# Two-layer hybrid encoder on one core: transposes of the heads' probabilities in runs of eight, a second value buffer, a second bank for the memory's products, later row classes in branch B, contiguous x

## The chip, the cores and the metric

The kernel runs on one core of a Trainium2 chip. TensorE (PE) multiplies and transposes, VectorE (DVE), ScalarE (ACT) and GpSimd (POOL) do the elementwise work, SyncE (SP) and ScalarE issue most DMAs. The metric is the device time of one execution in microseconds; lower is better.

## The reference

The reference is two layers of an encoder over 512 tokens of width 1024, float32, with 256 memory tokens that are normalised once and used by both layers.

```
mem_n = rms_norm(mem, mem_norm_g)
for l in range(DEPTH):                       # DEPTH = 2
    h = rms_norm(x, g_pre_mix[l])
    q_a,k_a,v_a, q_b,k_b,v_b, q_m, gate_pre = split(h @ w_in[l])
    o_a = neighborhood_attention(q_a, k_a, v_a, rpb_na[l])   # 6 heads of 64, windows of 8 x 16
    o_b = dilated_attention(q_b, k_b, v_b)                   # 3 groups of 2 heads, mixed by denominators
    o_m = memory_attention(q_m, mem_n, w_mem_kv[l])          # 4 heads, 256 memory tokens
    gates = sigmoid(gate_pre + b_gate[l])
    merged = gates[0]*(o_a @ w_br_a[l]) + gates[1]*(o_b @ w_br_b[l]) + gates[2]*(o_m @ w_br_m[l])
    x = x + rms_norm(merged @ w_out[l], g_post_mix[l])
    u = depthwise_conv(rms_norm(x, g_pre_ffn[l]) @ w_up[l])  # width 3, D_FF = 2816
    a, b = split(u)
    x = x + rms_norm((gelu(a) * b) @ w_down[l], g_post_ffn[l])
```

## The kernel before, in words

All activations lie transposed, channels on partitions: x is eight tiles of 128 channels by 512 tokens, in two halves of 256 tokens. A float32 product is made of three products of rounded parts: each weight tile `wraw` and each activation is split in a high part (a CAST on ScalarE: `whi`, `h_111`, `m`) and a low part (a subtraction on VectorE: `wlo`, `h_112`), and TensorE adds hi·hi, hi·lo and lo·hi in one PSUM bank. In the listings h with odd numbers 111 to 125 are the high parts of the eight normalised channel tiles and the even ones their low parts; `h_95`, `h_97` and so on with a second number are tiles in which x is scaled before the split.

The banks of PSUM are pools: three "mm" banks for products, two "s" banks for scores, two "pt" banks for transposes (`tbank`), one "o" bank for a head's values. A tile of a pool waits until the instructions that read the bank's last tile are done. The same holds for buffers in SBUF: "sq" (line 324, 585, 674) is one buffer, in which `a_v` and `b_v` put a value tile before it is transposed.

The program is written by a small planner, the class `Woven`. It counts a nominal clock `clk` of TensorE's work. Attention heads, normalisations and value transposes are generators ("jobs") that are spawned with a delay. A job yields a number (the nominal microseconds until its next part is due) or a flag that it needs. While a projection is written, `tick` runs every job that is due. So the yields set where a job's parts stand between the projection's products, and TensorE executes strictly in the written order. The other engines execute in the order in which their instructions were placed, too, so a part that is placed earlier stands ahead of others on every engine. `ready(t)` makes the yield at least as long as the nominal backlog of ScalarE and VectorE.

Layer 0 begins with `load_x` for both halves (256 KB per DMA, line 196), a first group of six projection tiles for each half (`run_group`: half 0 first, then half 1, 48 products of 0.12 us for each pair of tiles), and the jobs `pre_norm_job` (half 1 with delay `SD1`) and `mem_norm_job` (delay 6.0). The latter loads the memory (line 460, on ScalarE's queue), squares it on ScalarE (`sq`), and adds the squares on VectorE; the sum goes through a product with a column of means. `mem_kv` then makes keys and values of the memory in four tiles. In the second layer its weights were loaded ahead (`pre`).

Branch A is six `a_head_job`s in each layer: scores of four windows in two parts, softmax (ScalarE's exponential, VectorE's RECIPROCAL and TENSOR_SCALAR), then eight 128 x 128 transposes of the probabilities `y` into two pt banks, each emptied by a CAST on ScalarE and a subtraction on VectorE, then the products with the values into the o bank. Branch B is four `b_job`s in each layer (two heads, two pairs of row classes): each class makes scores in both s banks, then three runs of four transposes follow. Branch M is four `m_head_job`s with two runs of four.

## Time and profile before

| | |
|---|---|
| time, median of 3 runs | 1542.07 us (1540.83 to 1543.23) |
| the profiled execution | 1541.12 us, its span 1539.3 us |
| TensorE busy | 1518.5 us, 99% of the span, 7970 products and transposes |
| VectorE, ScalarE, GpSimd busy | 941.2, 713.2 and 122.9 us |
| DMA | 149.23 MB, 97 GB/s over the span |
| granted TensorE clock | 0.998 |

In rows of the timeline the first number is the start in us from the span's beginning, the second the duration, then engine, line, operation, output<-inputs, shape, count; in brackets the idle time before it and whose work ended it. Line 114 is a helper through which all ScalarE and VectorE work is issued, line 252 issues all products, line 263 all transposes.

### The profile page before, as it was taken

The page shows a single profiled execution, that of the slowest core. Times are in us where ns is not written, and L with a number is a line of the kernel's source. Part 1 is how long each engine was busy: PE and PEld are TensorE (multiplying, and loading weights), DVE is VectorE, ACT ScalarE, POOL GpSimd, SP SyncE. Part 2 cuts the span into 40 slices and gives each one's busy share as a digit, 9 for nine tenths or more (in the row PEclk, how much of TensorE's full clock was granted, in tenths as well). Part 3 has the DMA queues.
Part 4 walks back from the last instruction along what each step waited for, and adds up shares of the span by engine and source line. Part 5 has one row for each costly group of instructions (what it writes and reads, how often), then busy time and mean ns, then how long its engine had stood idle before and what let it go on. Part 6 is the DMA issues. An engine that isn't in the chain of part 4 may idle for free.

```text
span 1539.3 us, 20627 instructions
## 1 busy us (share of the span) xinstructions
PE 1518.5 (99%) x7970; PEld 1297.4 (84%) x7970; DVE 941.2 (61%) x1686; ACT 713.2 (46%) x1272; POOL 122.9 (8%) x191
## 2 busy tenths in 40 slices
PE   8999999999999999999999999999999999999997
PEld 7988888888988888888898888888889888888887
DVE  6685676335777777633387856743457877776233
ACT  5565554235544444533366655533355544444231
POOL 3220000220000000010044100012100000000000
PEclk9999999999999999999999999999999999999999
DMA  7331113224212222333362221132350233223331
GB/s 254 95 110 62 62 57 100 92 95 153 67 56 96 96 97 96 120 100 97 116 178 81 85 71 57 59 116 75 116 164 15 90 100 98 96 96 90 99 104 64
DMA packets 47490, 149.23 MB, mean 97 GB/s; under 512 B 5648, under 2 KB 9872, under 8 KB 47392
## 3 DMA queue, kind: packets, MB, share of 16 engines
q1 hardware_dynamic: 43632, 139.46, 28.4%
q0 software_dynamic: 2464, 6.36, 1.7%
q10 hardware_dynamic: 1296, 2.10, 0.4%
q8 instruction: 62, 1.02, 0.3%
q14 instruction: 36, 0.29, 0.1%
HBM read 145.80 MB, written 2.10 MB: 96 GB/s over the span
## 4 chain that ended last, share of the span: by engine, by line
PE 94%; DVE 3%; ACT 1%; issue 1%; DMA 0%; SPq 0%; ACTq 0%
PE mm L252 82%; PE s L252 5%; PE o L252 4%; PE pt L263 2%; PE pt L252 1%; DVE m L114 1%; DVE y L114 1%; DVE ka L114 0%; DMA x<-in_xT_dram 0%; ACT y L114 0%; DVE wlo L114 0%; DVE h L114 0%; DVE st L114 0%; ACT whi L114 0%; PE pt L347 0%
## 5 line engine op out<-in xcount | busy, mean ns | idle before, releaser
L252 PE MATMUL mm<-h,whi 128*128 128x512 f32 x2496 | 775.6, 392 | 0.0
L252 PEld LDWEIGHTS mm<-h,whi 128*128 128x128 f32 x2496 | 461.5, 188 | 91.0
L252 PE MATMUL mm<-h,wlo 128*128 128x512 f32 x1248 | 486.5, 390 | 0.0
L114 DVE TENSOR_TENSOR wlo<-wraw,whi 128x1024 fp32r<-128x1024 f32 (+1 forms) x213 | 258.3, 1213 | 284.7 <-ACT whi L114 282.0
L114 ACT CAST whi<-wraw 128x1024 fp32r<-128x1024 f32 (+1 forms) x213 | 221.1, 1038 | 307.8 <-PE mm L252 292.9
L252 PEld LDWEIGHTS mm<-h,wlo 128*128 128x128 f32 x1248 | 234.2, 188 | 49.7
L252 PE MATMUL mm<-m,whi 128*128 128x512 f32 (+1 forms) x800 | 215.1, 356 | 0.9 <-DVE m L114 0.8
L252 PEld LDWEIGHTS mm<-m,whi 128*128 128x128 f32 x800 | 141.8, 189 | 22.8 <-PE mm L252 1.3
L252 PE MATMUL mm<-m,wlo 128*128 128x512 f32 (+1 forms) x400 | 142.2, 355 | 0.0
L114 DVE SCALAR_TENSOR_TENSOR y<-y,vec,y 128x511 f32<-128x511 f32 x176 | 130.4, 747 | 3.5 <-ACT y L114 0.9
L114 DVE TENSOR_TENSOR y<-mm,R 128x512 f32<-128x512 f32 x82 | 56.3, 687 | 68.5 <-PE mm L252 68.5
L252 PEld LDWEIGHTS mm<-m,wlo 128*128 128x128 f32 x400 | 75.5, 189 | 10.9
L114 ACT ACTIVATE y<-y,vec 128x512 f32<-128x512 f32 x88 | 71.0, 813 | 2.1 <-DVE y L114 1.9
L804 POOL TENSOR_TENSOR m<-m,y 128x512 f32<-128x512 f32 x28 | 36.1, 1288 | 399.5 <-DVE y L114 399.5
L252 PE MATMUL mm<-m,m 128*128 128x512 f32 x240 | 63.5, 394 | 0.0
L114 ACT ACTIVATE y<-y 128x512 f32<-128x512 f32 x44 | 27.8, 632 | 72.0 <-DVE y L114 71.5
L114 ACT CAST m<-pt 128x512 fp32r<-128x512 f32 (+1 forms) x72 | 38.5, 540 | 46.2 <-PE pt L263 36.3
L114 DVE TENSOR_TENSOR m<-pt,m 128x512 fp32r<-128x512 f32 (+1 forms) x72 | 45.0, 629 | 20.7 <-ACT m L114 19.5
L114 ACT ACTIVATE y<-y,st 128x256 f32<-128x256 f32 (+1 forms) x80 | 43.6, 546 | 28.6 <-DVE st L114 25.8
L114 DVE TENSOR_TENSOR acc<-acc,sq 128x256 f32<-128x256 f32 (+1 forms) x80 | 38.1, 477 | 26.3 <-ACT sq L114 24.4
L114 ACT CAST m<-y 128x512 fp32r<-128x512 f32 x32 | 19.8, 619 | 72.5 <-DVE y L114 72.5
L114 DVE TENSOR_TENSOR m<-wraw,m 128x512 fp32r<-128x512 f32 (+1 forms) x60 | 38.4, 653 | 22.8 <-ACT m L114 22.7
(157 smaller groups left out, 1765.4 us busy)
## 6 DMA issues: line engine op xcount, KB each, us to landing
wraw<-in_w_in_dram SPq DMA_DIRECT2D x88, 512.0 KB, 3.7
wraw<-in_w_up_dram SPq DMA_DIRECT2D x88, 512.0 KB, 3.7
wraw<-in_w_down_dram SPq DMA_DIRECT2D x32, 512.0 KB, 3.5
wraw<-in_w_out_dram SPq DMA_DIRECT2D x16, 512.0 KB, 4.2
wraw<-in_w_down_dram SPq DMA_DIRECT2D x16, 384.0 KB, 3.2
wraw<-in_w_kv_dram SPq DMA_DIRECT2D x8, 512.0 KB, 4.1
y<-in_rpb_dram POOLq DMA_DIRECT2D x12, 256.0 KB, 3.5
wraw<-in_w_bra_dram SPq DMA_DIRECT2D x16, 192.0 KB, 2.3
```

The costliest lines, as they stand in the source:

```text
L114: return op(*args, **kw)
L252: wv.pe(nc.tensor.matmul(ps, a, b, start=first, stop=last), cost)
L263: wv.pe(nc.tensor.transpose(ps[:, 128 * i:128 * i + 128], s, ident), 0.11)
L804: (V if br == 2 and m >= 6 else G).tensor_add(acc[m], acc[m], gs)
```

## The change

Seven edits. `SD1`, the delay of half 1's normalisation job, goes from 4.0 to 5.0. x is laid out so that each 256 KB DMA reads one contiguous piece of DRAM (before: 128 rows of 2 KB, 16 KB apart). The "sq" pool gets two buffers. Odd tiles of the memory's keys and values go to a pt bank in layer 0. In `a_head_job` and `m_head_job` there is no yield between the two runs of transposes. In `b_job` the second row class yields at least the backlog of the engines, and there is no yield behind the first run of transposes.

```diff
--- before.py
+++ after.py
@@ -36,7 +36,7 @@
 LAT_QK, LAT_SM, LAT_T, LAT_V, LAT_T2 = 1.0, 4.5, 1.5, 2.0, 0.6
 STEP_A, STEP_B, STEP_M = 9.0, 9.0, 5.5
 SQG, LOG, GEN, KVE = {0: (), 1: ()}, {0: (), 1: ()}, 'DVVGVG', 'VVDD'
-SD1 = 4.0
+SD1 = 5.0
 MARGIN = 0.3
 SB = True
 TAILG = (0, 2, 4, 6)
@@ -193,7 +193,7 @@
     def load_x(half):
         for k in range(0, KD, 2):
             i = half.start // 256
-            nc.sync.dma_start(out=xs[:, i, k:k + 2, :], in_=xT[:, i, k:k + 2, :])
+            nc.sync.dma_start(out=xs[:, i, k:k + 2, :], in_=xT[i, k // 2])
 
     g0 = const.tile([128, KD], F32, name="g0")
     nc.scalar.dma_start(out=g0, in_=vecs[:, 0, V_PRE:V_PRE + KD])
@@ -321,7 +321,7 @@
             ACT.activation(acc, src, AF.Square)
         else:
             n = acc.shape[-1]
-            sq = slot((128, 256)) if slot else small("sq2", 4) if n == 256 else small("sq", 1, (128, 512))
+            sq = slot((128, 256)) if slot else small("sq2", 4) if n == 256 else small("sq", 2, (128, 512))
             ACT.activation(sq, src, AF.Square)
             (eng or V).tensor_add(acc, acc, sq)
 
@@ -485,7 +485,7 @@
         wv.need(f"mem{l}")
         for m in range(4):
             w = pre[m] if pre else weights(w_kv[l, m], KD, 128)
-            ps = mmbank((128, N_MEM))
+            ps = (mmbank if pre or m % 2 == 0 else tbank)((128, N_MEM))
             linear(ps, w, hm, slice(0, N_MEM))
             if m < 2:
                 t, u = big(F32R, (128, 2, N_MEM)), big(F32R, (128, 2, N_MEM))
@@ -582,7 +582,7 @@
 
     def a_v(ps, qkv, flag):
 
-        vT = small("sq", 1, (128, 512))
+        vT = small("sq", 2, (128, 512))
         ps3 = ps.rearrange("p (r c) -> p r c", r=8)
         vv = vT.rearrange("p (j r c) -> p j r c", j=4, r=8)
         ACT.copy(vv[:, 1:4], ps3[:, :, 8:56].rearrange("p r (j c) -> p j r c", j=3))
@@ -623,7 +623,6 @@
             yield LAT_QK if bp == 0 else ready(LAT_SM)
         c0, c1 = slice(0, 128), slice(128, 256)
         t0 = transpose_split([P[0][:, c0], P[3][:, c1], P[0][:, c1], P[1][:, c0]])
-        yield ready(LAT_T2)
         t1 = transpose_split([P[1][:, c1], P[2][:, c0], P[2][:, c1], P[3][:, c0]])
         yield ready(LAT_T)
         po = obank(128)
@@ -671,7 +670,7 @@
         qkv[1].append(kk)
 
     def b_v(g, ps, qkv, flag):
-        vT = small("sq", 1, (128, 512))
+        vT = small("sq", 2, (128, 512))
         if g == 0:
             ACT.copy(vT, ps)
         else:
@@ -706,12 +705,13 @@
             V.tensor_scalar_mul(S1[:, c2, :], S1[:, c2, :], d0)
             P.append([S[:, 128 * i:128 * i + 128] for i in range(4)]
                      + [S1[:, c2, 128 * i:128 * i + 128] for i in range(2)])
-            yield LAT_QK if c2 == 0 else ready(LAT_SM)
+            yield ready(LAT_QK if c2 == 0 else LAT_SM)
         tt = []
         for i in range(3):
             tt.append((transpose_copy if i == 2 else transpose_split)(
                 [P[c2][2 * i + a] for a in range(2) for c2 in range(2)]))
-            yield ready(LAT_T2) if i < 2 else ready(LAT_T)
+            if i > 0:
+                yield ready(LAT_T2 if i == 1 else LAT_T)
         for kt in range(4):
             off = 256 * (kt % 2)
             mm_values(po, vs[0][kt][sl], [t[:, off:off + 256] for t in tt[kt // 2]],
@@ -755,7 +755,8 @@
         tt = []
         for kt in range(2):
             tt.append(transpose_split([P[q][:, 128 * kt:128 * kt + 128] for q in range(4)]))
-            yield ready(LAT_T2) if kt == 0 else ready(LAT_T)
+            if kt == 1:
+                yield ready(LAT_T)
         po = obank(128)
         for kt in range(2):
             mm_values(po, vm[pr][:, kt, h % 2], tt[kt], lambda t: t, kt == 0, kt == 1, 512)
@@ -1066,7 +1067,7 @@
         return v.reshape(L, -1, 128)
 
     a = {}
-    a["xT"] = np.ascontiguousarray(g["x"][0].T.reshape(KD, 128, 2, 256).transpose(1, 2, 0, 3))
+    a["xT"] = np.ascontiguousarray(g["x"][0].T.reshape(4, 2, 128, 2, 256).transpose(3, 0, 2, 1, 4))
     a["memT"] = np.ascontiguousarray(g["mem"][0].T.reshape(KD, 128, N_MEM).transpose(1, 0, 2))
     a["memg"] = np.ascontiguousarray(g["mem_norm_g"].reshape(KD, 128).T)
     vec = np.concatenate([cols(g["g_pre_mix"]), cols(g["g_post_mix"]), cols(g["g_pre_ffn"]), cols(g["g_post_ffn"]),
```

The numbers of instructions on each engine are the same as before. What moves is the order. On ScalarE, in the first 40 us, the casts of half 1's high parts (h_115 to h_125) stood between the memory's loads and ahead of its squares (sq, from m tiles 385 to 391):

```order
L114 CAST h_119<-h_87_369 128x256
L460 DMA m_387<-in_memT_dram 128x512
L460 DMA m_389<-in_memT_dram 128x512
L114 CAST h_121<-h_88_373 128x256
L114 CAST h_123<-h_89_377 128x256
L114 CAST h_125<-h_90_381 128x256
L460 DMA m_391<-in_memT_dram 128x512
L114 ACTIVATE h_95_393<-m_385 128x256
L114 ACTIVATE sq_96_395<-m_385 128x256
L114 ACTIVATE sq_97_398<-m_387 128x256
L114 ACTIVATE sq_98_401<-m_387 128x256
```

After the change the same stretch reads:

```order
L114 ACTIVATE sq_89_364<-m_353 128x256
L114 ACTIVATE sq_90_367<-m_353 128x256
L114 ACTIVATE sq_91_370<-m_355 128x256
L114 ACTIVATE sq_92_373<-m_355 128x256
L114 ACTIVATE sq_93_376<-m_357 128x256
L114 CAST h_111<-h_95_390 128x256
L114 ACTIVATE sq_94_379<-m_357 128x256
L114 CAST h_113<-h_96_394 128x256
L114 CAST whi_700<-wraw_698 128x1024
L114 CAST whi_741<-wraw_739 128x1024
L114 CAST h_115<-h_97_398 128x256
L114 CAST h_117<-h_98_402 128x256
```

The memory's four loads and eight squares now stand ahead of the second half's casts, and two weight casts (whi, for the memory's keys) between them. VectorE in the same stretch, before; h_122 to h_126 are low parts of half 1, the rows with h_95_393 add up the memory's squares:

```order
L114 TENSOR_TENSOR h_122<-h_88_373,h_121 128x256
L114 TENSOR_TENSOR h_124<-h_89_377,h_123 128x256
L114 TENSOR_TENSOR h_126<-h_90_381,h_125 128x256
L114 TENSOR_TENSOR h_95_393<-h_95_393,sq_96_395 128x256
L114 TENSOR_TENSOR h_95_393<-h_95_393,sq_97_398 128x256
L114 TENSOR_TENSOR h_95_393<-h_95_393,sq_98_401 128x256
L114 TENSOR_TENSOR h_95_393<-h_95_393,sq_99_404 128x256
L114 TENSOR_TENSOR h_95_393<-h_95_393,sq_100_407 128x256
L114 TENSOR_TENSOR h_95_393<-h_95_393,sq_101_410 128x256
L114 TENSOR_TENSOR h_95_393<-h_95_393,sq_102_413 128x256
L114 TENSOR_TENSOR wlo_701<-wraw_698,whi_700 128x1024
L114 TENSOR_TENSOR wlo_742<-wraw_739,whi_741 128x1024
```

And after; the memory's sum is now h_87_359, and scalings of x (SCALAR_TENSOR_TENSOR) and low parts follow behind:

```order
L114 TENSOR_TENSOR h_112<-h_95_390,h_111 128x256
L114 TENSOR_TENSOR h_87_359<-h_87_359,sq_92_373 128x256
L114 TENSOR_TENSOR h_114<-h_96_394,h_113 128x256
L114 TENSOR_TENSOR h_87_359<-h_87_359,sq_93_376 128x256
L114 SCALAR_TENSOR_TENSOR h_97_398<-x,g_86,pt_337 128x256
L114 TENSOR_TENSOR h_87_359<-h_87_359,sq_94_379 128x256
L114 SCALAR_TENSOR_TENSOR h_98_402<-x,g_86,pt_337 128x256
L114 TENSOR_TENSOR wlo_701<-wraw_698,whi_700 128x1024
L114 TENSOR_TENSOR h_116<-h_97_398,h_115 128x256
L114 TENSOR_TENSOR h_118<-h_98_402,h_117 128x256
L114 SCALAR_TENSOR_TENSOR h_99_406<-x,g_86,pt_337 128x256
L114 SCALAR_TENSOR_TENSOR h_100_410<-x,g_86,pt_337 128x256
```

Of half 1 two low parts (h_112, h_114) now stand among the memory's sums, and h_116 to h_126 behind the first subtraction of memory weights, wlo_701, some also behind the second, wlo_742.

The second place is the first layer's head 0 on VectorE: y_1012 and y_1036 are its four probability tiles, m_1106 the low part of its first bank of transposes. Before:

```order
L114 TENSOR_SCALAR y_1012<-y_1012,st_1021 128x256
L114 TENSOR_SCALAR y_1036<-y_1036,st_1039 128x256
L114 RECIPROCAL st_1045<-st_1045 128x1
L114 TENSOR_SCALAR y_1036<-y_1036,st_1045 128x256
L114 SCALAR_TENSOR_TENSOR ka_1054<-mm_965,ka_1052 64x512
L114 TENSOR_TENSOR wlo_1119<-wraw_1116,whi_1118 128x1024
L114 SCALAR_TENSOR_TENSOR ka_1055<-mm_965,ka_1053 64x512
L114 TENSOR_TENSOR m_1106<-pt_1100,m_1105 128x512
```

After:

```order
L114 TENSOR_SCALAR y_1012<-y_1012,st_1021 128x256
L114 TENSOR_SCALAR y_1036<-y_1036,st_1039 128x256
L114 SCALAR_TENSOR_TENSOR ka_1054<-mm_965,ka_1052 64x512
L114 TENSOR_TENSOR wlo_1128<-wraw_1125,whi_1127 128x1024
L114 RECIPROCAL st_1045<-st_1045 128x1
L114 SCALAR_TENSOR_TENSOR ka_1055<-mm_965,ka_1053 64x512
L114 TENSOR_SCALAR y_1036<-y_1036,st_1045 128x256
L114 TENSOR_TENSOR m_1106<-pt_1100,m_1105 128x512
L114 TENSOR_TENSOR m_1115<-pt_1109,m_1114 128x512
```

The last normalisation (RECIPROCAL and TENSOR_SCALAR with st_1045) now stands behind a key and a weight subtraction, and the two banks of transposes, pt_1100 and pt_1109, are emptied one directly after the other.

The third place is TensorE at the last job of branch B in layer 0: y_2284 and y_2331 hold the probabilities of its row classes, y_2283 the rest of them, o_2181 takes the values. Before:

```order
L263 MATMUL pt_2400<-ident,y_2284 128x128
L263 MATMUL pt_2400<-ident,y_2331 128x128
L263 MATMUL pt_2400<-ident,y_2284 128x128
L263 MATMUL pt_2400<-ident,y_2331 128x128
L252 MATMUL mm_2411<-m_1190,m_2317 128x512
L252 MATMUL mm_2411<-m_1191,m_2317 128x512
L252 MATMUL mm_2411<-m_1190,m_2318 128x512
L252 MATMUL mm_2411<-m_1438,m_2317 128x512
L252 MATMUL mm_2411<-m_1439,m_2317 128x512
L252 MATMUL mm_2411<-m_1438,m_2318 128x512
L263 MATMUL pt_2418<-ident,y_2283 128x128 x4
L252 MATMUL mm_2411<-m_1660,m_2317 128x512
```

After, with y_2311, y_2353 and y_2310 in the same parts:

```order
L252 MATMUL mm_2393<-m_1658,m_2278 128x512
L252 MATMUL mm_2393<-m_1657,m_2279 128x512
L263 MATMUL pt_2403<-ident,y_2311 128x128
L263 MATMUL pt_2403<-ident,y_2353 128x128
L263 MATMUL pt_2403<-ident,y_2311 128x128
L263 MATMUL pt_2403<-ident,y_2353 128x128
L263 MATMUL pt_2412<-ident,y_2311 128x128
L263 MATMUL pt_2412<-ident,y_2353 128x128
L263 MATMUL pt_2412<-ident,y_2311 128x128
L263 MATMUL pt_2412<-ident,y_2353 128x128
L263 MATMUL pt_2422<-ident,y_2310 128x128 x4
L252 MATMUL o_2181<-m_2408,m_1472 128x256
```

The three runs of transposes stood apart, with products between them; now twelve stand in one run, on two pt banks.

## The prediction

> **What bounds the kernel now.** I read the page first: busy time, the slices, the chain.
>
> ```profile
> PE 1518.5 (99%) x7970; PEld 1297.4 (84%) x7970; DVE 941.2 (61%) x1686; ACT 713.2 (46%) x1272; POOL 122.9 (8%) x191
> PE 94%; DVE 3%; ACT 1%; issue 1%; DMA 0%; SPq 0%; ACTq 0%
> ```
>
> TensorE is busy for 99% of the span and 94% of the chain, and the change removes none of its products. So what can be won is TensorE's idle time, 1539.3 − 1518.5 = 20.8 us, and what can be lost is new idle time. A table of windows says where it lies (start:end, length, then busy time of each engine, granted clock, DMA share, GB/s):
>
> ```profile
> 0.00:17.00 17.00, 11.76 (x35) 7.99 (x35) 7.39 (x18) 8.48 (x20) 5.42 (x34) 1.00 0.80 269
> 17.00:36.00 19.00, 18.07 (x141) 17.87 (x142) 15.59 (x37) 12.57 (x33) 7.70 (x8) 1.00 0.75 267
> 36.00:62.00 26.00, 25.16 (x210) 24.98 (x210) 16.74 (x33) 12.78 (x27) 7.79 (x13) 1.00 0.21 66
> 62.00:135.00 73.00, 72.06 (x405) 61.80 (x404) 57.18 (x151) 47.07 (x110) 14.94 (x24) 1.00 0.32 102
> 135.00:222.00 87.00, 86.14 (x459) 71.48 (x458) 49.94 (x113) 42.57 (x83) 0.00 (x0) 1.00 0.21 65
> ...
> 780.00:895.00 115.00, 112.80 (x733) 101.65 (x733) 92.11 (x229) 69.26 (x162) 33.77 (x65) 1.00 0.33 102
> 895.00:1006.00 111.00, 109.94 (x589) 91.38 (x588) 73.76 (x172) 59.06 (x129) 0.00 (x0) 1.00 0.19 60
> 1006.00:1515.00 509.00, 509.00 (x2509) 431.75 (x2507) 286.20 (x400) 210.47 (x307) 18.03 (x14) 1.00 0.30 95
> 1515.00:1540.00 25.00, 15.76 (x131) 15.35 (x130) 10.48 (x31) 2.02 (x6) 3.20 (x4) 0.89 0.26 85
> ```
>
> Start (5.2 us idle) and tail (9.2, of which 0.7 is behind the span's end) hold two thirds. The second layer's gate and MLP stage idles 0.0 us in 509 (the first layer's, left out, reads alike). The attention stages, which nearly all of the edits touch, idle 0.84 + 0.94 + 0.86 + 2.20 + 1.06 = 5.9 us. That caps what the attention edits can win at about 6 us, 0.4%. The next fence lists these waits: TensorE's rows of the timeline (start, duration, in brackets the idle time before and who ended it), and two lines of line 263's own waits (total, count).
>
> ```profile
> 22.61 1.05 PE L252 MATMUL pt<-mean,y 128*128 128x1 f32 x8 [0.90 <-DVE y L114]
> 59.63 0.28 PE L252 MATMUL mm<-m,wlo 128*128 128x256 f32 x1
> 60.76 0.47 PE L252 MATMUL mm<-m,whi 128*128 128x256 f32 x2 [0.84 <-DVE m L114]
> ...
> 76.28 0.66 PE L263 MATMUL pt<-ident,sq 128*128 128x128 f32 x4 [0.80 <-ACT sq L114]
> ...
> 172.48 0.71 PE L252 MATMUL s<-m,m 128*128 128x128 f32 x4 [0.46 <-DVE st L114]
> ...
> 864.58 0.55 PE L263 MATMUL pt<-ident,y 128*128 128x128 f32 x3 [1.26 <-DVE y L114]
> ...
> 949.82 1.17 PE L252 MATMUL s<-m,m 128*128 128x512 f32 x6 [0.37 <-DVE st L114]
>   ACT sq L114: 1.7, 2
>   DVE y L114: 1.3, 1
> ```
>
> The product behind the one at 59.63 would have come 0.12 us later (half of a 0.24 us step), and came 1.13 later: a wait of 0.84 costs 1.0, so each wait loses about 0.17 us beside its idle time. I add that everywhere.
>
> **The gains.** (1) Memory products: the third product waits for the only free bank. With odd products in a transpose bank it starts at once: −1.0. The weights it needs are a copy and subtraction that end by 59.3, so nothing else is late there. (2) Value buffers: the second run of value transposes waits for ScalarE's copy into the single "sq" tile, twice, 1.7 us: −(1.7 + 2 × 0.17) = −2.0. (3) Second layer, 864.58: a head's transposes come up before its fourth probability tile is normalised. With the run of eight placed later this goes: −(1.3 + 0.17) = −1.5. (4) Row classes of B: the second class of a job waits for the score bank that the first still holds. There are four such rows (two a layer, 0.46 and 0.37 each, first and last shown): −(1.66 + 4 × 0.17) = −2.3. (5) The wait at 22.61 may lose its 0.90, since that product moves some rows back; but what TensorE gains there it waits for in the next stage (below): 0. (6) Runs of eight: 28 runs of four join another.
>
> ```profile
> 85.96 0.60 PE L263 MATMUL pt<-ident,y 128*128 128x128 f32 x4
> 86.31 0.71 PE L252 MATMUL mm<-h,whi 128*128 128x512 f32 x2
> ...
> 87.10 0.62 PE L252 MATMUL mm<-h,whi 128*128 128x512 f32 x2
> ```
>
> The product behind a run starts 0.35 after it, and its pair takes 0.71 instead of 0.62: 0.44 in all for four transposes, or 0.11 each, so that a longer run wins next to nothing. Bounds 0 and −0.09 for each of 28; taken −0.2, at the near end. Gains: −7.0.
>
> **The first stage, where SD1 acts.** The order of ScalarE and VectorE shows that the memory's squares and their sums now stand ahead of the normalised second half of x. Rows of that stretch, ACT, then DVE, then PE:
>
> ```profile
> 27.66 0.33 ACTq L460 DMA_DIRECT2D m<-in_memT_dram  x1
> 29.52 0.82 ACTq L460 DMA_DIRECT2D m<-in_memT_dram  x2
> 32.92 0.33 ACTq L460 DMA_DIRECT2D m<-in_memT_dram  x1
> 34.47 0.42 ACT L114 ACTIVATE h<-m 128x256 f32<-128x256 f32 x1 [1.15 <-DMA m<-in_memT_dram]
> 34.79 1.04 ACT L114 ACTIVATE sq<-m 128x256 f32<-128x256 f32 x3
> 38.12 0.72 ACT L114 ACTIVATE sq<-m 128x256 f32<-128x256 f32 x2 [1.19 <-DMA m<-in_memT_dram]
> ```
>
> ```profile
> 31.63 1.25 DVE L114 SCALAR_TENSOR_TENSOR h<-x,g,pt 128x256 f32<-128x256 f32 x3
> 32.80 1.08 DVE L114 TENSOR_TENSOR h<-h,h 128x256 fp32r<-128x256 f32 x3
> 35.22 2.54 DVE L114 TENSOR_TENSOR h<-h,sq 128x256 f32<-128x256 f32 x5 [1.34 <-ACT sq L114]
> 39.81 2.36 DVE L114 TENSOR_TENSOR wlo<-wraw,whi 128x1024 fp32r<-128x1024 f32 x2 [0.29 <-ACT whi L114]
> ```
>
> ```profile
> 36.05 5.20 PE L252 MATMUL mm<-h,m 128*128 128x256 f32 x42
> ```
>
> Before, all eight pairs of h are done at 33.9 and TensorE reaches them at 36.05 without a wait. Now ScalarE can square only when the memory lands. With squares from 34.47 at 0.32 us each, VectorE's four sums (0.5 each) end at 36.9, the first h (0.34) at 37.3, then a sum, h, a sum, a scaling (0.4), a sum and a scaling bring 39.9, the first wlo (1.2) 41.1, two h and two scalings 42.6, the second wlo 43.8, two h and two scalings 45.3; the last pair waits for its copy on ScalarE (0.4) and ends near 46.4. TensorE's product with that last h stands 43 steps of 0.12 into the group, at 41.2 now. Late end: 46.4 − 41.2 = +5.2. Early end: the four loads issue together (27.7 to 28.7), and the quickest of the four takes 38.1 − 32.9 = 5.2 us, so squares could begin at 32.9: +3.6. I take +4.5, nearer the late end, since the first load issues no earlier than before and three more now share the queue with it. No other work of TensorE stands there as cover: the group is in order.
>
> **The other losses.** (a) First layer, head 0: one scaled key copy and one weight copy now stand ahead of the fourth exponential, and a 1.2 to 1.6 us wlo ahead of the last normalisation.
>
> ```profile
> 82.49 0.50 ACT L114 ACTIVATE y<-y,st 128x256 f32<-128x256 f32 x1
> ...
> 83.45 1.04 ACT L114 CAST whi<-wraw 128x1024 fp32r<-128x1024 f32 x1
> ```
>
> ```profile
> 83.40 0.35 DVE L114 TENSOR_SCALAR y<-y,st 128x256 f32<-128x256 f32 x1
> ...
> 84.53 1.56 DVE L114 TENSOR_TENSOR wlo<-wraw,whi 128x1024 fp32r<-128x1024 f32 x1 [0.18 <-ACT whi L114]
> 87.27 0.69 DVE L114 TENSOR_TENSOR m<-pt,m 128x512 fp32r<-128x512 f32 x1 [0.45 <-ACT m L114]
> ```
>
> The last normalisation, at 83.40 now, comes behind the weight work, near 86.5 to 87.1. The eighth transpose wants it at 85.96 + 7 × 0.11 = 86.7, and by then TensorE runs up to 2 us earlier (gains 1 and 2). Bounds 0 and +1.6; taken +1.0. (b) Two transpose banks: a run of eight fills both, and each is free only when ScalarE and VectorE have emptied it (85.96 to 87.96 above, 2.0 us). Where a value transpose or a third run stands right behind, it waits. The order has that at some six places of branch A, at 0 to 0.7 each: taken 0.3, +1.8. (c) In B's last job of each layer the three runs now stand one behind another, so the third waits for the first bank: 2.0 less two runs (2 × 0.44) is 1.1, less what is spared before; bounds 0 and 1.1 each, taken 0.5: +1.0. (d) M's heads: their stages idle little (the window 895:1006 holds 1.06, 0.83 of it B's), bounds −0.2 and +0.5, taken 0.
>
> **Contiguous x.** The number of packets and their 2 KB stay; only their pitch in memory changes.
>
> ```profile
> 7.11 1.41 ACT L114 ACTIVATE y<-x 128x256 f32<-128x256 f32 x4 [2.08 <-DMA x<-in_xT_dram]
> ```
>
> ScalarE waits 2.08 us for the second part of x, so the edit could win up to that and, if it ties up the queue, lose as much; in this stretch the DMA engines are 80% busy at 269 GB/s over 17 us, with weights in the same queue, and that work isn't less. And in the next stage TensorE waits for h at a time set by the memory's landing, so an earlier start would mostly be waited off there. Taken 0. The Trainium skill (DMA: Bandwidth & Descriptors, "Latency and other measured facts") says that rows at a pitch of 512 KiB and above slow a copy, and that contiguous tiles restore it; the pitch here is 16 KiB, so by that rule nothing changes either, and if it held already here the sum would be up to 2 us lower, 1540.4.
>
> **Sum.** 1541.1 (the profiled run's own time: span 1539.3 and 1.8 around it; the median is 0.95 above, inside the 2.4 of the three runs) − 7.0 + 4.5 + 1.0 + 1.8 + 1.0 = 1542.4. Within 0.2%, 3.1 us, I call it the same: about what a measurement of this kernel can tell from no change.
>
> **Rivals.** *Faster, the new waits are covered* (a, b and c cost nothing, since VectorE and ScalarE, 61% and 46% busy, keep ahead of TensorE): 1542.4 − 3.8 = 1538.6. It decides where an evacuation of a bank, 2.0 us above, has other products of that length beside it. The share of busy time speaks for it, the places where two runs follow each other against. Chance 0.19. *Faster, x lands sooner*: 1540.4, under 1539 only with part of the other; the 2.08 wait speaks for it, the 80% and the wait for the memory against. Chance 0.06. *Slower, B's jobs stall on the third run*: with a class later by 1.4 us the run of the last eight transposes meets the evacuation in all eight jobs, not two, at 0.7 each: 1542.4 − 1.0 + 5.6 = 1547.0. It decides from a distance of under 2.0 us between second and third run; in most jobs three products and four scores (1.6 us) stand there, which is close. Chance 0.14. *The change doesn't do what it says in B* (the second class still waits, since VectorE's chain moved with it): +2.3, 1544.7. Chance 0.12. *Forecast*, about the same at 1542.4: 0.49.
>
> **How the numbers follow.** Faster is the first rival, half of the second: 0.19 + 0.03, and 0.05 of the forecast's own edge (the early landing): 0.27. Slower is the third, half of the fourth and 0.04 of the edge: 0.24. Same: 0.49. The range runs from the first rival less 0.8 for half of the bounds of the first stage, 1537.8, to the third, 1547.0; outside of it I leave all together some 2 in 10.
>
> **What would show it.** A wait of several us in TensorE's rows from 36 to 46 with releaser "DVE h" confirms the first stage; none there makes the prediction 4.5 too high. The waits at 60.76, 76.28, 172.48, 864.58 and 949.82 should be gone; new ones "pt" behind "DVE m" should stand in 62 to 222 and 780 to 1006. The windows 222:780 and 1006:1515 should read as now, shifted. If x lands earlier, the row at 7.11 does. Wrong would be the whole sum if memory lands so early that the squares cost nothing, or if the shifted orders of VectorE meet TensorE at places that the walk by hand did not reach.

## The result, and the profile after

The changed kernel is slower: 1550.86 us median of 4 runs (1550.43 to 1553.65) against 1542.09 us (1540.83 to 1543.23), ratio 1.0062 [1.0049, 1.0075]. The forecast was 1542.4, with 1547.0 as its upper end. The profiled execution took 1550.43 us, its span 1548.7 us. Busy times and the chain hardly moved; TensorE now has 26.9 us without work (1548.7 − 1521.8) instead of 20.8:

```profile
PE 1521.8 (98%) x7970; PEld 1300.5 (84%) x7970; DVE 941.5 (61%) x1686; ACT 711.7 (46%) x1272; POOL 123.7 (8%) x191
PE 92%; DVE 5%; ACT 1%; DMA 1%; issue 1%; SPq 0%; ACTq 0%; DVEq 0%
```

VectorE's share of the chain went from 3 to 5%: it is what TensorE now waits for. The windows of before, without the tail (columns as before):

```profile
0.00:17.00 17.00, 11.32 (x37) 7.81 (x38) 7.96 (x19) 8.53 (x20) 5.58 (x34) 0.72 0.82 278
17.00:36.00 19.00, 18.03 (x134) 17.62 (x133) 10.13 (x23) 9.91 (x26) 7.50 (x8) 0.90 0.77 262
36.00:62.00 26.00, 24.23 (x183) 23.24 (x182) 18.69 (x42) 12.53 (x32) 5.15 (x8) 0.93 0.14 45
62.00:135.00 73.00, 70.41 (x405) 60.60 (x404) 55.34 (x135) 46.24 (x102) 16.31 (x26) 1.00 0.32 102
135.00:222.00 87.00, 85.26 (x451) 71.32 (x449) 50.37 (x125) 41.74 (x85) 1.05 (x2) 1.00 0.20 63
222.00:780.00 558.00, 555.75 (x2737) 469.90 (x2738) 328.27 (x491) 244.55 (x389) 27.40 (x24) 1.00 0.31 97
780.00:895.00 115.00, 114.82 (x774) 105.11 (x773) 95.49 (x236) 72.57 (x171) 38.39 (x70) 1.00 0.38 117
895.00:1006.00 111.00, 109.03 (x588) 91.35 (x587) 72.73 (x176) 59.20 (x132) 1.05 (x2) 1.00 0.19 58
1006.00:1515.00 509.00, 507.96 (x2468) 428.87 (x2467) 291.44 (x413) 213.55 (x312) 18.04 (x14) 1.00 0.31 97
```

Read them with the shift in mind: TensorE runs some 9 us late from 260 us on, so a window's end cuts the stage earlier than before. Two things stand out. In 36:62 TensorE does 183 products instead of 210, though it idles only 0.9 us more. The granted clock is 0.93 there: from 41.5 to 44.9 products come every 0.21 us instead of every 0.12, so that time in which TensorE would otherwise stand and wait for h reads as busy. (The clock of the first two windows, 0.72 and 0.90, can't be compared with the 1.00 of before; the last section says why.) And 780:895, a stage of attention, idles 0.18 instead of 2.20. The gains came, and were outweighed elsewhere. In the timeline the first stage of the changed kernel reads (TensorE's first product of the memory's keys is the last row; before the change it began at 53.99):

```profile
36.89 2.03 PE L252 MATMUL mm<-h,m 128*128 128x256 f32 x12
39.71 0.38 PE L252 MATMUL mm<-h,m 128*128 128x256 f32 x1 [0.79 <-ACT h L114]
40.95 5.46 PE L252 MATMUL mm<-h,m 128*128 128x256 f32 x29 [0.86 <-DVE h L114]
...
59.15 0.40 PE L252 MATMUL mm<-m,whi 128*128 128x256 f32 x2
```

```profile
34.17 0.42 ACT L114 ACTIVATE h<-m 128x256 f32<-128x256 f32 x1 [5.10 <-DMA m<-in_memT_dram]
```

```profile
34.93 2.01 DVE L114 TENSOR_TENSOR h<-h,sq 128x256 f32<-128x256 f32 x4 [7.13 <-ACT sq L114]
...
39.34 1.22 DVE L114 TENSOR_TENSOR wlo<-wraw,whi 128x1024 fp32r<-128x1024 f32 x1
...
41.93 1.22 DVE L114 TENSOR_TENSOR wlo<-wraw,whi 128x1024 fp32r<-128x1024 f32 x1
...
44.68 0.82 DVE L114 TENSOR_TENSOR h<-h,h 128x256 fp32r<-128x256 f32 x2
```

ScalarE waits 5.10 us for the memory and begins to square at 34.17. VectorE stands idle for 7.13 us until the squares come, makes four sums, and then gives out half 1's low parts between the weight subtractions; the last pair is done at 45.5. TensorE enters the group at 36.89 and creeps through it: it is 5.2 us late when it reaches the memory's keys. From there on these waits are new; the old ones at 60.76, 76.28, 172.48, 864.58 and 949.82 have no counterpart:

```profile
90.23 0.99 PE L263 MATMUL pt<-ident,y 128*128 128x128 f32 x7 [1.18 <-DVE y L114]
104.75 1.40 PE L252 MATMUL o<-m,m 128*64 128x256 f32 x7 [0.46 <-DVE m L114]
123.39 0.63 PE L263 MATMUL pt<-ident,y 128*128 128x128 f32 x4 [0.74 <-DVE m L114]
145.60 0.66 PE L263 MATMUL pt<-ident,sq 128*128 128x128 f32 x4 [0.96 <-DVE m L114]
183.38 1.78 PE L252 MATMUL o<-m,m 128*64 128x256 f32 x11 [0.74 <-DVE m L114]
222.93 0.66 PE L263 MATMUL pt<-ident,y 128*128 128x128 f32 x4 [0.96 <-DVE m L114]
237.51 0.69 PE L252 MATMUL o<-m,m 128*64 128x512 f32 x2 [0.27 <-DVE m L114]
251.68 0.45 PE L252 MATMUL o<-m,m 128*64 128x512 f32 x1 [0.38 <-DVE m L114]
252.80 0.68 PE L252 MATMUL o<-m,m 128*64 128x512 f32 x2 [0.67 <-DVE m L114]
```

These are layer 0; those of branches B and M (from 183) repeat in layer 1 at 755.5 us later. Three kinds are seen: transposes that wait for a probability (y), transposes that wait for a bank (pt behind m), and values that wait for the parts of what was just transposed (o behind m). The transposes at 145.60 are those of a value tile (sq) that stands directly behind a run of eight.

### The profile page after: what moved, and what is told of

The parts are those of the page before. It is cut to its first block, busy times and chain, and to the rows that moved or that the text cites. A ratio compares the mean times of both kernels' runs of the same rounds, so it can differ in the third digit from the quotient of the medians.

```text
span 1548.7 us, 20623 instructions
## 1 busy us (share of the span) xinstructions
PE 1521.8 (98%) x7970; PEld 1300.5 (84%) x7970; DVE 941.5 (61%) x1686; ACT 711.7 (46%) x1272; POOL 123.7 (8%) x191
## 4 chain that ended last, share of the span: by engine, by line
PE 92%; DVE 5%; ACT 1%; DMA 1%; issue 1%; SPq 0%; ACTq 0%; DVEq 0%
PE mm L252 81%; PE s L252 4%; PE o L252 3%; PE pt L263 2%; PE pt L252 1%; DVE m L114 1%; DVE y L114 1%; DVE wlo L114 1%; DVE h L114 1%; ACT m L114 1%; ACT y L114 0%; DMA x<-in_xT_dram 0%; DVE st L114 0%; DMA wraw<-in_w_in_dram 0%; DMA m<-in_memT_dram 0%
## 5 line engine op out<-in xcount | busy, mean ns | idle before, releaser
L252 PE MATMUL mm<-m,whi 128*128 128x512 f32 (+1 forms) x768 | 209.1, 359 | 0.0
L252 PEld LDWEIGHTS mm<-m,whi 128*128 128x128 f32 x768 | 136.9, 189 | 21.5
L252 PE MATMUL mm<-m,wlo 128*128 128x512 f32 (+1 forms) x384 | 137.6, 358 | 0.0
L252 PEld LDWEIGHTS mm<-m,wlo 128*128 128x128 f32 x384 | 72.4, 189 | 10.9
L114 DVE TENSOR_TENSOR m<-pt,m 128x512 fp32r<-128x512 f32 (+2 forms) x74 | 44.0, 621 | 15.4 <-ACT m L114 14.7
L252 PE MATMUL mm<-h,m 128*128 128x256 f32 x312 | 49.6, 301 | 3.8 <-ACT h L114 1.8
```

Source lines behind the costliest of these rows:

```text
L114: return op(*args, **kw)
L252: wv.pe(nc.tensor.matmul(ps, a, b, start=first, stop=last), cost)
```

## The experiments

The prediction left three causes to be told apart: the order of the first stage, the runs of eight, and (seen only in the profile after) the lowered clock at the start. Each time is the median of the kernel's runs, each ratio (with its 95% interval) goes against the kernel before on the same chip. The experiments ran on several chips, on which the kernel before took 1541.8 to 1543.0 us, so medians of different experiments can be compared only to about 1 us. For small differences the traces say more. TensorE makes the same products in all of these kernels, so the time between two of them can be compared from trace to trace; a stretch in which nothing was changed mostly agrees to 0.1 us, but for the start and the join between the layers.

**1. SD1 back** (in the changed kernel).

```diff
-SD1 = 5.0
+SD1 = 4.0
```

> The changed kernel with SD1 = 4.0 again. Theory 'order' (the loss lies where the new order makes TensorE wait): half 1 of x reaches TensorE without a wait, the memory products start 5.2 us earlier (59.15 to about 54), and the time falls by 4.5 to 5.5, from 1550.9 to about 1546. Theory 'clock' (the loss is the half clock that was granted in some windows before 56 us, caused by TensorE's idle start): the windows that lie before 28 us stay, so the time falls by 2 at most, to 1549.

Measured: 1545.30 us, ratio 1.0018 [1.0008, 1.0028], by the medians 5.6 less than the changed kernel, by the ratios 6.8. TensorE reaches half 1 at 34.37 and passes it without a wait, and reaches the memory's keys at 52.31 instead of 59.15, 6.8 earlier. That is more than the 5.2 against the kernel before, because TensorE also began 1.7 earlier than there (first product with h at 10.79 instead of 12.47), and nothing waits that off now. The row of half 1, and the clock:

```profile
34.37 5.20 PE L252 MATMUL mm<-h,m 128*128 128x256 f32 x42
...
7.00:18.00 11.00, 8.37 (x35) 7.21 (x36) 8.77 (x22) 6.21 (x16) 1.45 (x1) 0.54 0.96 348
```

The granted clock is 0.54 in 7:18 of this profile, as low as in the changed kernel (0.53), and its first stage is the fast one all the same.

**2. SD1 = 5.0 alone** (in the kernel before).

```diff
-SD1 = 4.0
+SD1 = 5.0
```

> The kernel before with SD1 = 5.0 as its only edit. Theory 'order': half 1's h comes at 45 to 46 us and TensorE, which was there at 36.05, loses 4.5 to 5.2 with nothing to hide it; the rest of the order is as before: 1542.1 + 5 = 1547. Theory 'interaction' (it cost only together with contiguous x and the other edits): within 1.5 of 1542.

Measured: 1548.17 us, ratio 1.0036 [1.0023, 1.0049]. That is +5.6 by the ratio, with nothing else changed. In its trace TensorE reaches the memory's keys 6.0 us later than in the kernel before and is 6.0 late from there on. The rows creep in the same way:

```profile
37.89 2.02 PE L252 MATMUL mm<-h,m 128*128 128x256 f32 x12 [0.70 <-ACT h L114]
40.70 0.38 PE L252 MATMUL mm<-h,m 128*128 128x256 f32 x1 [0.79 <-ACT h L114]
41.94 5.31 PE L252 MATMUL mm<-h,m 128*128 128x256 f32 x29 [0.85 <-DVE h L114]
```

So the one number SD1 makes more than half of the loss, and it does not need the other edits for it.

**3. The old layout of x** (in the changed kernel; the diff, with the array in DRAM laid out to match), and **4. contiguous x alone** (in the kernel before; the same edit the other way round).

```diff
-            nc.sync.dma_start(out=xs[:, i, k:k + 2, :], in_=xT[i, k // 2])
+            nc.sync.dma_start(out=xs[:, i, k:k + 2, :], in_=xT[:, i, k:k + 2, :])
```

> The changed kernel with the old layout of x. Theory 'order': the start moves back by 0.6 us, but TensorE waits for the second half's h at 36 to 45 us in any case, so the time stays within 1 us of 1550.9. Theory 'clock': the granted clock is 0.998 again as before the change, and the time falls to about 1543.

> The kernel before with contiguous x as its only edit. If the earlier start seen in the other runs (first product with h at 10.8 to 11.9 instead of 12.4 to 12.5) comes from the layout, nothing waits it off while half 1's h is ready at 33.9: 1542.1 - 0.6 to 1.6, about 1541. If the layout does nothing and the start scatters: 1542.1 +- 0.5 with the first product with h at 12.4.

Measured with the old layout: 1554.44 us, 1.0072 [1.0057, 1.0087], not told apart from the changed kernel. The clock of 7:18 is still 0.54, so neither half of the theory "clock" holds: the low clock doesn't come from the layout, and the time didn't fall. Its profiled execution (1555.08) is 4.7 behind the changed kernel's, and 3.3 of that come between the layers, where TensorE waits (1.13 of it idle at 790.97) for a sum of squares of x; ScalarE had waited 2.29 there for a weight to land. Experiment 10's trace loses 1.9 at the same place, and most others next to nothing. What decides it was not tested.

Contiguous x alone: 1540.57 us, 0.9993 [0.9984, 1.0002]: not told apart from no change either. In its trace the first product with h comes at 10.80, TensorE is 1.7 us ahead of the kernel before through the first layer and 1.4 ahead at the end. So an earlier start is kept, as expected; whether the layout makes it is a question of the last section.

**5. The yield back in M's heads**, and **6. the run of eight kept there, with a longer yield behind it** (both in the changed kernel).

Experiment 5:

```diff
-            if kt == 1:
-                yield ready(LAT_T)
+            yield ready(LAT_T2) if kt == 0 else ready(LAT_T)
```

Experiment 6:

```diff
-                yield ready(LAT_T)
+                yield ready(LAT_T + 1.5)
```

> The changed kernel with the yield between the two runs of transposes in M's heads again. Theory 'order': the three waits of values behind a run of eight in each layer (236.85, 250.90, 251.68: 1.9 together, against 0.4 before) go, -3.0 in both layers: 1547.9. Theory 'clock': unchanged, 1550.9.

> The changed kernel with the run of eight in M's heads kept, and 1.5 nominal us more between it and the values (LAT_T + 1.5). Theory 'distance' (the run is harmless, only the yield behind it was left as short as for one bank): the value waits of M (1.9 in each layer) go as in m_back, 1548.2. Theory 'run' (eight transposes at a time cost whatever the distance, since the waits move to the next scores or transposes): 1550.9 or more.

Measured: 1548.41 us, 1.0034 [1.0021, 1.0047], and 1548.55 us, 1.0041 [1.0027, 1.0055]. By the medians both take away about 2.4 us; by the intervals the first is just told apart from the changed kernel (1.0062 [1.0049, 1.0075]), the second is not. The traces show the place: the changed kernel takes 1.5 us longer for M in each layer than the kernel before, experiment 5 the same time as before, and experiment 6 even 0.6 and 0.5 less. In the second, the values behind a run of eight run through (TensorE's row of the head that waited twice at 251.68 and 252.80):

```profile
254.22 1.08 PE L252 MATMUL o<-m,m 128*128 128x512 f32 x4
```

So the run of eight as such cost M nothing; the distance behind it did. VectorE of the changed kernel, and TensorE's first product with the values, show why it was too short:

```profile
249.43 1.21 DVE L114 TENSOR_TENSOR wlo<-wraw,whi 128x1024 fp32r<-128x1024 f32 x1
...
250.95 0.67 DVE L114 TENSOR_TENSOR m<-pt,m 128x512 fp32r<-128x512 f32 x1
...
252.06 0.68 DVE L114 TENSOR_TENSOR m<-pt,m 128x512 fp32r<-128x512 f32 x1
```

```profile
250.90 0.40 PE L252 MATMUL o<-m,m 128*128 128x512 f32 x1
```

Both banks' subtractions stand behind a weight subtraction, with normalisations of the next head between them. TensorE's values begin at 250.90 with the high part and want the low parts with the second and third product, 0.23 and 0.45 later; they come at 251.62 and 252.74.

**7. The yield back in A's heads** (in the changed kernel).

```diff
         t0 = transpose_split([P[0][:, c0], P[3][:, c1], P[0][:, c1], P[1][:, c0]])
+        yield ready(LAT_T2)
```

> The changed kernel with the yield between the two runs of transposes in branch A's heads again. Theory 'run' (a run of eight fills both transpose banks, so what comes next, values or the next transposes, waits until ScalarE and VectorE have emptied them): the waits at 88.79 (1.39), 103 to 105 (1.27), 122.37 (0.96) and 144.36 (1.18) in layer 0 go, -4.8, and the wait of 1.47 in layer 1 that the change had removed comes back: 1547.6. Theory 'memory first' (nothing but the wait for half 1, 5.2, is real, the rest is scatter): unchanged, 1550.9.

Measured: 1549.70 us, 1.0052 [1.0038, 1.0065], only 1.2 less, and by the intervals not told apart from the changed kernel. Its trace tells the two layers apart. In layer 0 the value wait and the bank waits (104.75, 123.39, 145.60) are gone, and branch A takes 2.9 us less than in the changed kernel; in layer 1 the wait for a probability is back (1.27 idle), and branch A takes 1.8 more. The run of eight is a loss in the one layer and a gain in the other. The wait of head 0 (1.21 idle) stands as before, so it is not the run's. VectorE of the changed kernel:

```profile
87.67 1.20 DVE L114 TENSOR_TENSOR wlo<-wraw,whi 128x1024 fp32r<-128x1024 f32 x1
...
89.71 0.47 DVE L114 TENSOR_SCALAR y<-y,st 128x256 f32<-128x256 f32 x1
```

The last normalisation follows a weight subtraction. It comes with the value buffers or the memory's bank, as experiment 10 shows without any run of eight; which of the two brings it was not tested.

**8. Branch B's job as before**, and **9. its later row class without the long run** (both in the changed kernel).

Experiment 8 (the lines between are left out):

```diff
-            yield ready(LAT_QK if c2 == 0 else LAT_SM)
+            yield LAT_QK if c2 == 0 else ready(LAT_SM)
...
-            if i > 0:
-                yield ready(LAT_T2 if i == 1 else LAT_T)
+            yield ready(LAT_T2) if i < 2 else ready(LAT_T)
```

Experiment 9:

```diff
-            if i > 0:
-                yield ready(LAT_T2 if i == 1 else LAT_T)
+            yield ready(LAT_T2) if i < 2 else ready(LAT_T)
```

> The changed kernel with branch B's job as before (both edits undone). Theory 'order': the waits of the run of twelve (221.69 and 977.16, 1.18 each) and of the values (182.35 and 937.82, 0.91 each) go, -4.2, and the four waits for a score bank come back, +2.3: 1549.0. Theory 'clock': 1550.9 + 2.3 or unchanged, since no low clock lies in branch B.

> The changed kernel with the yield behind the first run of branch B again, and the later second row class kept. Theory 'run': the waits at 221.69 and 977.16 (1.18 each) and of the values (0.91 each) go, and the four score-bank waits (2.3) stay away: 1546.7. Theory 'class' (the later class pushes the job's values towards the next part, and with it comes the 0.91): 1548.5.

Measured: 1550.13 us, 1.0047 [1.0032, 1.0062], and 1552.16 us, 1.0062 [1.0047, 1.0077]. Neither is told apart from the changed kernel. In the first the waits changed places as expected: branch B of layer 0 takes 0.8 us less than in the changed kernel, the same as before the change. The second missed both theories. With the yield restored, the later class isn't free either: its probabilities come late for the first run of transposes, and the values behind them wait too:

```profile
189.32 0.55 PE L263 MATMUL pt<-ident,y 128*128 128x128 f32 x3 [0.56 <-DVE y L114]
...
221.24 0.55 PE L263 MATMUL pt<-ident,y 128*128 128x128 f32 x3 [0.65 <-DVE y L114]
...
225.84 1.35 PE L252 MATMUL o<-m,m 128*64 128x256 f32 x9 [0.34 <-DVE m L114]
```

**10. Value buffers and memory bank alone** (in the kernel before).

```diff
-            ps = mmbank((128, N_MEM))
+            ps = (mmbank if pre or m % 2 == 0 else tbank)((128, N_MEM))
...
-        vT = small("sq", 1, (128, 512))
+        vT = small("sq", 2, (128, 512))
```

The second edit is shown at one of three places.

> The kernel before with the two value buffers and the memory tiles in a transpose bank alone. Theory 'order': -1.25 (memory tiles) - 2.1 (value buffers), and the head 0 wait of 1.4 (the last normalisation behind weight work) appears, since it is in every kernel that has these two, with and without a run of eight: 1540.2. Without that wait: 1538.8.

Measured: 1539.88 us, 0.9984 [0.9976, 0.9992], with the wait of head 0 (the profiled execution, 1543.59, is the slowest of the twelve; what it loses besides stands at experiment 3 and in the last section):

```profile
87.59 0.55 PE L263 MATMUL pt<-ident,y 128*128 128x128 f32 x3 [1.18 <-DVE y L114]
```

**11. The four edits without long runs**: value buffers, memory bank, contiguous x and the later class, SD1 and all yields as before.

> The kernel before with four of the edits: two value buffers, odd memory tiles in a transpose bank, contiguous x, the later second row class (all yields between runs and SD1 = 4.0 as before). Theory 'order': 1542.1 - 1.25 (memory tiles) - 2.1 (value buffers) - 2.3 (classes) - 1.0 (earlier start) = 1535.5. Theory 'scatter': within 2 of 1542.

Measured: 1540.73 us, 0.9992 [0.9983, 1.0000]. The expectation missed by 5. In the trace the later class costs 0.9 in each layer's branch B, with waits for probabilities and values as in experiment 9 (0.59, 0.64 and 0.34 in layer 0), instead of gaining 2.3 in all; and head 0's wait (1.14) had been left out of the sum.

**12. The useful parts**: value buffers, memory bank, contiguous x, the run of eight in A in layer 1 only, and a longer yield ahead of head 0's transposes in layer 0.

The two edits in `a_head_job` against the changed kernel (the others, as above, are left out):

```diff
-            yield LAT_QK if bp == 0 else ready(LAT_SM)
+            yield LAT_QK if bp == 0 else ready(LAT_SM) + (1.5 if l == h == 0 else 0.0)
...
+        if l == 0:
+            yield ready(LAT_T2)
```

> The kernel before with value buffers, memory tiles, contiguous x, a run of eight in branch A in layer 1 only, and 1.5 nominal us more ahead of the transposes of layer 0's head 0. Theory 'order': 1542.1 - 1.25 - 2.1 - 0.6 - 1.0 (layer 1's wait of 1.47 goes, two small ones come) = 1537.2, without the head 0 wait. Otherwise the head 0 wait stays, 1538.6.

Measured: 1537.90 us, 0.9967 [0.9955, 0.9979], between the two expectations. In its trace head 0's wait for a probability is gone, and a wait for values stands in its place:

```profile
89.33 0.80 PE L252 MATMUL o<-m,m 128*64 128x256 f32 x5 [0.48 <-DVE m L114]
```

**13. All runs of eight with longer yields**, SD1 back (in the changed kernel).

```diff
-SD1 = 5.0
+SD1 = 4.0
-LAT_QK, LAT_SM, LAT_T, LAT_V, LAT_T2 = 1.0, 4.5, 1.5, 2.0, 0.6
+LAT_QK, LAT_SM, LAT_T, LAT_V, LAT_T2 = 1.0, 4.5, 3.0, 2.0, 2.1
```

> The changed kernel with SD1 = 4.0, all runs of eight kept, and 1.5 nominal us more behind every run of transposes (LAT_T 3.0, LAT_T2 2.1). Theory 'distance' (only the yields behind the runs are too short for two banks): from 1545.3 (SD1 back) the value waits of A (1.27), B (0.9 x 2) and M (1.9 x 2) go and the run of twelve (1.18 x 2) is pulled apart, -9.2; head 0's wait and the third-run waits of A (3.5) stay: about 1537. Theory 'run' (the waits only move to the next scores or transposes): 1544 or more.

Measured: 1540.71 us, 0.9990 [0.9980, 0.9999]: by the medians 4.6 less than SD1 back, half of the 9.2 expected. All value waits are gone. The bank wait of the twelve (third run) stays, and a new wait for probabilities has come:

```profile
182.31 0.98 PE L263 MATMUL pt<-ident,y 128*128 128x128 f32 x7 [0.65 <-DVE y L114]
...
216.70 0.66 PE L263 MATMUL pt<-ident,y 128*128 128x128 f32 x4 [0.97 <-DVE m L114]
```

So both theories hold for a part. What the values wait for is the distance. The twelve were not pulled apart: in this trace, too, the third run stands directly behind the eight, although the yield between is longer. Wherever twelve stand in one run, in the traces of the changed kernel and of experiments 1, 7 and 13, the third run waits 0.96 or 0.97 us for the first bank.

**14. The same as 12, with B's second class at 1.8** instead of 1.0 nominal us.

```diff
-            yield LAT_QK if c2 == 0 else ready(LAT_SM)
+            yield 1.8 if c2 == 0 else ready(LAT_SM)
```

> The kernel best2 with B's second row class at 1.8 nominal us instead of 1.0, a fixed distance between the 1.0 before and the engines' backlog in the changed kernel. If the wait for the score bank (0.6 each, four) can be had without new waits: 1537.9 - 2.3 = 1535.6. If any later class pushes the transposes and values together, as the changed one did: 1538 to 1539.

Measured: 1534.83 us, 0.9958 [0.9945, 0.9970]. This is the fastest of these kernels. Against experiment 12 the intervals overlap, but the profiled executions differ by 2.0 us (1534.37 and 1536.34), and 1.6 of these lie in the two layers' branch B: its stages no longer hold a wait for a score bank. The first stage and branch B of layer 0 read:

```profile
36.00:62.00 26.00, 26.00 (x220) 26.00 (x219) 17.02 (x32) 12.74 (x29) 8.53 (x13) 1.00 0.19 62
...
135.00:222.00 87.00, 86.62 (x464) 72.55 (x462) 51.27 (x121) 43.64 (x87) 0.00 (x0) 1.00 0.21 65
```

The first stage idles 0.00 us, of 0.84 before, and 0.38 us idle remain in 135:222, of 0.86 before. A later class does give its gain, at the right size.

## Why the prediction was wrong, point by point

Where the time went can be read between the same products of TensorE in the two traces (changed kernel less kernel before, us; the stretches end near the ends of the stages). The forecast's terms are put in the stretches where they belong:

| stretch | measured | forecast |
|---|---|---|
| start, to the first product with h | −0.6 | 0 |
| first stage, to the memory's keys | +5.8 | +4.5 |
| the memory's keys | −1.3 | −1.0 |
| branch A, both layers (+3.2 and −2.8) | +0.4 | −0.7 |
| branch B, both layers (+0.8 and +1.2) | +2.0 | −1.3 |
| branch M, both layers (+1.5 in each) | +3.0 | 0 |
| shorter transposes in longer runs | | −0.2 |
| all | +9.3 | +1.3 |

Of the 8.0 us that were missed, 3.3 lie in branch B, 3.0 in M and 1.1 in A.

**The first stage** was forecast at +4.5, between 3.6 and 5.2. With the start it took 5.2 in the trace of the changed kernel, 6.0 alone (experiment 2) and 6.8 where an earlier start would have been kept (experiment 1). The mechanism and the walk were right: the last h was put at 46.4 and came at 45.5, and at 45.8 to 47.8 in the other profiles with SD1 = 5.0. The term was at least 0.7 too small, since the early landing didn't come: squares began at 34.2, 0.3 earlier than before.

**The gains** 1 to 4 are all in the trace: the five old waits are gone. The memory's keys won 1.3 instead of 1.0. As a gain in time, the first two are shown (experiment 10, −2.5 with head 0's wait against them). That x would change nothing in this kernel stands as not told apart; that an earlier start is waited off in it is borne out, since the memory's keys come at 59.2 to 61.0 with SD1 = 5.0, whenever TensorE began.

**Head 0** (a), forecast +1.0: 1.18 idle, right. **Third runs in A** (b), forecast six times 0.3, 1.8: two of 0.74 and 0.96, 2.1 with their restarts. The sum is right by luck, with a third of the places at about three times the price. **The twelve** (c), forecast 0.5 a layer, cost 0.96 idle each and 1.1 with the restart: the upper end of its bounds; the term was mis-sized by 0.6 in each layer.

**The step that failed** is (d) and what it stands for: "M's heads … taken 0", and no line at all for the values behind a run of eight in A and B. By the rows above these cost 0.46 in A, 0.74 in B and 1.32 in M, the last two again in layer 1, and each restart some 0.17 more: 0.6 + 2 × 0.9 + 2 × 1.8 = 6.0, against 2 × 0.4 before the change. That is 5.2 us, and the forecast with it, with the 0.7 of the first stage and 1.3 for the twelve, would have come to 1549.6; the profiled execution took 1550.4. Experiments 5 and 6 bear the largest part out: M's 1.5 in each layer go when the yield between the runs returns, and also when the run stays and the values come later. The prediction had the price in hand: it wrote that a bank is free 2.0 us after its run begins, and charged that to the next transposes alone. The values need the second bank's low part, one subtraction and whatever stands between later, and the yield ahead of them had stayed at 1.5.

**The rivals.** That the banks empty in time (0.19) is refuted by the waits behind "DVE m". The slower rival named the right direction and the wrong place: B's third run waits in one job of four, not in all. That gain 4 might not come proved half true: the waits for the score bank went, and 0.74 and 0.96 came elsewhere in branch B (experiment 8).

**The clock** is not the cause. Experiment 1 shows the same low clock in 7:18 as the changed kernel and is 5.6 us faster by the medians, and experiment 4 shows it too (0.53) at 1540.57; the last section shows that the kernel before has it as well. The half clock from 41.5 to 44.9 in the changed kernel cost 0.4 at most: from the last h to the memory's keys it takes 13.65 us, and 13.26 in experiments 3, 5 and 9, which have the full clock there.

## What to carry to other kernels

In a kernel that is bound by one engine in written order, an edit of a delay is priced by what it moves on the other engines: one step of SD1 put the memory's landing ahead of work that TensorE needed first, and cost more than all the buffers won. When two transposes' banks are filled in one run, lengthen the distance to everyone who reads them, the values too, and keep products between it and a third run, as the kernel before did. A later start of B's second class was worth 1.6 us at one size (1.8) and cost 1.8 at another (the engines' whole backlog, experiment 11): try the size before the rule.

## What the runs showed of the hardware

The clock column of the windows reads 1.00 from the start in the kernel before and in experiments 11, 12 and 14, and about 0.54 in 7:18 of the changed kernel. That is not a difference in speed. Line 252's products of 15.0 to 17.1 us, in the kernel before and in the changed one (columns PE, weight loads, clock, DMA share, GB/s):

```profile
15.00:17.10 2.10, 2.00 (x10) 1.71 (x9) 1.00 0.81 259
```

```profile
15.00:17.10 2.10, 2.00 (x10) 1.71 (x9) 0.50 0.76 240
```

Both do ten products in 2.0 us busy, one every 0.21 us, where a later group does one every 0.12. In all sixteen profiles products come every 0.21 us up to 16.0 to 19.4 us and every 0.12 us behind that. The trace's record of the clock begins only with its first change, which is at 19.2 in the kernel before, and the column (and with it the mean of 0.998) counts what lies ahead of it as 1.00. So every kernel here runs at half clock when its first products with h come. After that ten profiles, all eight with SD1 = 5.0 among them, show one or two more stretches of half clock before 46 us, each 3.4 or 6.8 us long (experiment 3's has one more, at 793). The Trainium skill (TensorE: Matmul & The Clock Gate, "What's actually happening") says that the clock halves after an idle window of about 3.4 us and that the windows run free of the kernel's start. The lengths here agree with it, and the free phase would fit that the release comes at 16.0 to 19.4 us in kernels with the same first instructions.

What the half clock costs depends on where it falls. From the first product with h to the memory's keys it takes 41.5 us in the six profiles with SD1 = 4.0 that have no later stretch, whether the release comes at 17.2 or at 19.4, so up to there the clock doesn't set the pace; TensorE waits for h in that stretch (1.01 and 0.91 idle at 12.47 and 13.96 in the kernel before). With a stretch of 3.4 us from 22.8 (experiment 13) or 25.3 (experiment 10), where TensorE has work, it takes 43.0: 1.5 more.

The first product with h started at 10.8 to 12.5 us in the twelve profiles with contiguous x (mean 11.4) and at 12.1 to 13.5 in the four with rows 16 KiB apart (mean 12.6). The Trainium skill (DMA: Bandwidth & Descriptors, "Latency and other measured facts") gives rates for row pitches of 512 KiB (207 GB/s) to 8 MiB (103 GB/s), against 214 GB/s where 4 MiB are padded by 4 KiB; no run here has such pitches. Whether the layout makes the 1.2 us is not settled, since the starts scatter by more than that and the whole time couldn't be told apart.
